# Seven products for eight: the up projection of two token blocks by Strassen's algorithm, and the down projection as a stage of its own

## The chip, the cores and the metric

One NeuronCore of a Trainium2 chip runs the whole program. The metric is the device time of one execution in microseconds (us). The kernel before was run three times: 2574.15, 2579.14 and 2577.27 us, median 2577.27 us.

## What is computed

One inference step of a decoder trunk of two layers. 1088 columns of activations (64 sample tokens of 8 sequences, then 1024 prompt tokens) of 1024 features pass through a mixer (layer 0: mLSTM heads beside a short convolution; layer 1: sliding-window attention) and, in each layer, through a gated ConvFFN. It is the FFN that matters here:

```python
def conv_ffn(h, prev, w_up, conv_w, w_down):
    u = h @ w_up                                  # 1024 -> 2 * 2816
    u, new_prev = causal_conv(u, prev, conv_w)    # depthwise, width 3, along the tokens
    g, a = jnp.split(u, 2, axis=-1)
    return (jax.nn.silu(g) * a) @ w_down, new_prev

x = x + g1 * y                                    # y of the mixer
h = rms_norm(x, norm2[l]) * (1 + sc2) + sh2
y, fp = conv_ffn(h, st_ffn[l], f_w_up[l], f_conv_w[l], f_w_down[l])
x = x + g2 * y
```

## The kernel before

**Number format.** All is float32. An operand of a product is split into a high part (a cast to the type that TensorE, PE, multiplies) and a low part (what the cast left out). A product is three passes: high by high, high by low, low by high (`PASS`). ScalarE (ACT) casts, VectorE (DVE) subtracts: `split` (L81) for activations, `wunit` (L92) for a weight unit of 128 x 1024, which SyncE (SP) has loaded into a staging tile `st` (3 buffers).

**Tiling.** The columns are three blocks, `BLK`: 384, 384 and 320. A feature tile f (0 to 21) has two parts, p = 0 (the gate's input g) and p = 1 (a). `mm_unit` (L148) is one product of a part with a block: 8 k tiles by three passes, 24 matmuls into one PSUM bank.

**The up projection.** `up` (L453) runs one tile and one block. For each part: 24 matmuls, then the halo. The convolution needs the two columns before the block, so the product of block 1 or 2 is written behind two columns that ACT copies from the bank of the block before (L466):

```python
mm_unit(ps[:, h:], c1 - c0, w[p], c0)
if bi < 2:
    halo[p] = bank("up")
    A.copy(out=halo[p][:, 0:2], in_=ps[:, n - 2:n])
```

The bank of the next block can take its product only after this copy. Then ACT scales (L469), DVE adds the two other taps (L485; L475 and L477 for the 64 sample columns of block 0), ACT takes the Silu (L488), DVE multiplies (L489), and `split` makes the operand of the down projection, which stays in SBUF in a tile `g` of all 1088 columns.

**The down projection** comes in between: after each two feature tiles, `down` (L492) adds their part of all eight output tiles m over the three blocks (6 matmuls a group, L501), and `gate_add` (L396, DVE, L403) adds each group times its gate to x, which stays in SBUF. In layer 0 the modulation units of the next layer (`ada`, L198) run between the groups. The last two tiles go block by block, so that the next layer's norm can begin; its blocks 1 and 2 are finished between the products of keys and values (`kv`, L1028).

**Order.** The program lists jobs with the weight units that each takes; units of the coming jobs are loaded and split ahead. A scheduler of the framework then fixes one order of instructions for each engine, which works through it in that order.

Of the kernel before, what the change touches and what calls it, by code (L numbers as in the profile page):

```python
# [17 lines left out]
KT = 8  # L18
# [15 lines left out]
WSLOT = 2048  # L34

# order of the first steps, see trunk()
# [11 lines left out]
def trunk(ctx: ExitStack, tc: tile.TileContext, I, O):  # L48
# [27 lines left out]
    # activations, feature major, as hi and lo parts: the input of each product  # L76
# [3 lines left out]
    # ---------------------------------------------------------------- weights  # L80
# [28 lines left out]
    def fetch(n):  # L109
        """splits units of the coming jobs until n are ready"""  # L110
        while len(ready) < n and fetched[0] < len(jobs):
            srcs = jobs[fetched[0]][0]
            if fetched[1] < len(srcs):
                ready.append(wunit(srcs[fetched[1]]))
                fetched[1] += 1
            else:
                fetched[0] += 1
                fetched[1] = 0
# [29 lines left out]
    def mm_unit(ps, n, w, c0):  # L148
        """ps[:, :n] = sum over the 8 k tiles of w_k^T h_k[:, c0:c0+n]"""
# [6 lines left out]
    def mm_tok(ps, ws, c0, k0=0, k1=KT):  # L156
        """ps = h[:, c0:c0+128]^T times 512 columns of weights"""
# [66 lines left out]
    # modulation units that run between other work, each loaded one turn ahead  # L224
    pend, loaded = [], []

    def later_units(which, tmp):
        for l, cb in which:
            for u, run in enumerate(ada(l, 8 * cb, 16, 8, tmp)):
                pend.append((I["w_ada"][l, cb:cb + 2, u], run))  # L230

    def pump():
# [3 lines left out]
        if pend:  # L236
            src, run = pend.pop(0)
            w = wscratch("wa")
            SY.dma_start(out=w.rearrange("p (u c) -> p u c", u=2), in_=src.rearrange("u p c -> p u c"))
# [7 lines left out]
    def rsqrt_(out, v, tmp):  # L247
        """out = v^-0.5 of v in SBUF (v > 0), refined by one Newton step"""
# [13 lines left out]
    def ring(new, n, uses):  # L262
        """temporaries of 386 columns, n to a tile, a new tile after so many of them"""
# [10 lines left out]
    class Norm:  # L274
        """h = rms(x) * norm * (1 + sc) + sh, block by block"""
# [7 lines left out]
        def square(self, k, bi, eng=None):  # L283
            """adds the squares of x's k tile to the block's sum"""
# [19 lines left out]
        def total(self, bi):  # L304
            """the sums in token major, where the root takes few columns"""
# [20 lines left out]
        def spread(self, bi):  # L326
            """the roots, the same on all partitions"""
# [14 lines left out]
        def sample(self, k, eng):  # L342
            """k tiles k and k + 1 of the sample columns, up to their split"""
# [10 lines left out]
        def apply(self, k, bi):  # L354
            """k tiles k and k + 1 of a block"""
# [1358 lines left out]
```

## Time and profile before

| | us |
|---|---|
| three runs | 2574.15, 2577.27, 2579.14 |
| profiled execution, span | 2578.1 |
| of it TensorE busy | 2516.1 (98%) |
| VectorE / ScalarE / GpSimd busy | 1569.3 / 860.1 / 292.3 |
| moved by DMA | 195.97 MB, 76 GB/s over the span |

The profiled execution is a run of its own; the time that the page gives for it is its span, and it lies between the three measured ones. "Busy" of PE means that a matmul was under way; matmuls are pipelined, so one lasts longer in a row (335 ns) than its distance to the next. A group of instructions has its idle time before it and what released it.

### The profile page before, as it was taken

Reading aid. Unit: us, or ns where it says so; the run is one execution under the profiler, and the core shown is the slowest. Engines: PE = TensorE matmul, PEld = TensorE weight load, DVE = VectorE, ACT = ScalarE, POOL = GpSimd, SP = SyncE. Lnnn points to the kernel's source line nnn. Section 1 sums busy time; section 2 is a strip of 40 time slices with the busy share of each in tenths; the row PEclk is TensorE's granted clock in tenths of the full one; section 3 lists DMA queues with packets and bytes.
Section 4 is the critical chain, followed back from the end, with each engine's and each line's share of the span. In section 5 each row is a group of like instructions: output and inputs, shape, how many; then the busy total and the mean of one; then the engine's idle time right before and its main releaser. Section 6 shows DMA issues by size and latency. Waiting matters only on the chain.

```text
span 2578.1 us, 40693 instructions
## 1 busy us (share of the span) xinstructions
PE 2516.1 (98%) x15899; PEld 2374.7 (92%) x15899; DVE 1569.3 (61%) x3700; ACT 860.1 (33%) x2182; POOL 292.3 (11%) x523
## 2 busy tenths in 40 slices
PE   6999999999999999999998989899999999999999
PEld 5988998999999999999997866699999999999999
DVE  7332326556666656566667788956756666666665
ACT  5102323345222223222225456635422222222231
POOL 2001014121000000000006431203100000000000
PEclk9999999999999999999998999999999999999999
DMA  7455315411322212221110221220111111111112
GB/s 262 164 170 188 116 54 159 144 50 42 99 66 82 82 59 82 74 66 50 41 47 15 85 67 42 70 65 34 50 34 49 50 42 42 50 50 33 50 42 76
DMA packets 78144, 195.97 MB, mean 76 GB/s; under 512 B 9321, under 2 KB 36745, under 8 KB 77409
## 3 DMA queue, kind: packets, MB, share of 16 engines
q1 hardware_dynamic: 72960, 179.65, 21.7%
q0 software_dynamic: 4416, 13.60, 1.4%
q8 instruction: 126, 2.06, 0.3%
q14 instruction: 66, 0.53, 0.1%
q10 hardware_dynamic: 576, 0.13, 0.0%
HBM read 178.55 MB, written 16.76 MB: 76 GB/s over the span
## 4 chain that ended last, share of the span: by engine, by line
PE 86%; DVE 9%; ACT 1%; DMA 1%; issue 1%; POOL 1%; SPq 0%; DVEq 0%; ACTq 0%; POOLq 0%
PE up L152 39%; PE dn L501 20%; PE pj L152 6%; PE op L152 5%; PE cv L152 5%; PE ada L198 2%; PE q L1028 1%; PE kv L1028 1%; PE vp L160 1%; DVE nt L368 1%; DVE p L1207 1%; DVE p L1223 1%; PE op L1134 1%; DVE h L381 1%; DVE n L293 1%
## 5 line engine op out<-in xcount | busy, mean ns | idle before, releaser
L152 PE MATMUL up<-h,w 128*128 128x384 f32 (+1 forms) x6336 | 1052.8, 327 | 0.0
L152 PEld LDWEIGHTS up<-h,w 128*128 128x128 f32 x6336 | 1046.1, 188 | 5.9 <-ACT u L473 5.0
L501 PEld LDWEIGHTS dn<-g,w 128*128 128x128 f32 x3168 | 524.4, 188 | 7.5 <-DVE x L403 4.2
L501 PE MATMUL dn<-g,w 128*128 128x384 f32 (+1 forms) x3168 | 531.0, 327 | 0.0
L485 DVE SCALAR_TENSOR_TENSOR y<-up,fcw,y 128x319 f32<-128x319 f32 (+3 forms) x528 | 300.2, 570 | 228.9 <-ACT y L469 148.4
L403 DVE SCALAR_TENSOR_TENSOR x<-dn,mod,x 128x320 f32<-128x320 f32 (+1 forms) x528 | 300.0, 571 | 123.9 <-PE dn L501 111.0
L95 ACT CAST w<-st 128x1024 fp32r<-128x1024 f32 x179 | 186.5, 1054 | 498.7 <-PE dn L501 373.2
L96 DVE TENSOR_TENSOR w<-st,w 128x1024 fp32r<-128x1024 f32 x179 | 219.2, 1235 | 113.6 <-ACT w L95 111.9
L469 ACT ACTIVATE y<-up,fcw 128x320 f32<-128x320 f32 (+1 forms) x264 | 145.3, 551 | 76.5 <-PE up L152 75.0
L152 PE MATMUL op<-h,w 128*128 128x384 f32 (+1 forms) x960 | 163.4, 331 | 0.0
L152 PEld LDWEIGHTS op<-h,w 128*128 128x128 f32 x960 | 160.3, 193 | 0.0
L82 ACT CAST g<-y 128x384 fp32r<-128x384 f32 x132 | 65.4, 496 | 269.3 <-DVE y L489 269.3
L152 PEld LDWEIGHTS pj<-h,w 128*128 128x128 f32 x864 | 141.9, 188 | 8.4 <-issue 5.0
L152 PE MATMUL pj<-h,w 128*128 128x384 f32 (+1 forms) x864 | 145.1, 327 | 0.0
L152 PEld LDWEIGHTS cv<-h,w 128*128 128x128 f32 x720 | 118.4, 188 | 10.9 <-issue 7.5
L152 PE MATMUL cv<-h,w 128*128 128x384 f32 (+1 forms) x720 | 123.7, 328 | 0.0
L475 DVE TENSOR_SCALAR y<-u,fcw 128x64 f32<-128x64 f32 x88 | 22.5, 256 | 157.5 <-ACT u L473 157.5
L1028 PE MATMUL q<-w,h 128*128 128x512 f32 x432 | 115.4, 408 | 0.6 <-DVE rq L1000 0.6
L479 POOL COPY fst<-u 128x16 f32<-128x16 f32 x88 | 22.8, 259 | 820.3 <-ACT u L473 820.3
L488 ACT ACTIVATE y<-y 128x384 f32<-128x384 f32 x132 | 67.2, 509 | 131.7 <-DVE y L485 68.3
L83 DVE TENSOR_TENSOR g<-y,g 128x384 fp32r<-128x384 f32 x132 | 70.5, 534 | 61.1 <-ACT g L82 61.1
L466 ACT COPY up<-up 128x2 f32<-128x2 f32 x176 | 25.6, 146 | 222.3 <-PE up L152 211.5
(316 smaller groups left out, 2389.3 us busy)
## 6 DMA issues: line engine op xcount, KB each, us to landing
st<-in_f_up SPq DMA_DIRECT2D x88, 512.0 KB, 3.6
wa<-in_w_ada SPq DMA_DIRECT2D x40, 1024.0 KB, 5.6
st<-in_f_down SPq DMA_DIRECT2D x44, 512.0 KB, 3.5
st<-in_w_in SPq DMA_DIRECT2D x22, 512.0 KB, 4.5
st<-in_w_out SPq DMA_DIRECT2D x16, 512.0 KB, 3.7
st<-in_w_qkv SPq DMA_DIRECT2D x12, 512.0 KB, 3.7
wr<-in_w_ada SPq DMA_DIRECT2D x11, 512.0 KB, 8.6
x<-in_xT SPq DMA_DIRECT2D x4, 1088.0 KB, 10.7
```

Source lines behind the costliest of these rows:

```text
L82: A.copy(out=dst_hi, in_=src)
L83: (eng or V).tensor_tensor(out=dst_lo, in0=src, in1=dst_hi.bitcast(F32), op=ALU.subtract)
L95: A.copy(out=w[:, 0, :], in_=s)
L96: V.tensor_tensor(out=w[:, 1, :], in0=s, in1=w[:, 0, :].bitcast(F32), op=ALU.subtract)
L152: PE.matmul(ps[:, :n], w[:, a, 128 * k:128 * k + 128], H[k][:, b, c0:c0 + n], start=(k == 0 and i == 0), stop=(k == KT - 1 and i == 2))
L198: PE.matmul(hold["ps"][32 * c:32 * c + 32, 0:32 * nf], M["c"][:, 9 * kt:9 * kt + 32], wk[:, c], start=(kt == 0), stop=(kt == KT - 1), tile ...
L403: V.scalar_tensor_tensor(out=x[:, o:c1], in0=ps[:, o - c0:n], scalar=gt[:, 0:1], in1=x[:, o:c1], op0=ALU.mult, op1=ALU.add)
L469: A.activation(out=y[:, o:n], in_=ps[:, o:n], func=AF.Copy, scale=cw[:, fi, 2:3])
L485: V.scalar_tensor_tensor(out=y[:, q:n], in0=ps[:, q - d:n - d], scalar=cw[:, fi, j:j + 1], in1=y[:, q:n], op0=ALU.mult, op1=ALU.add)
L488: A.activation(out=a, in_=a, func=AF.Silu)
L501: PE.matmul(ps[:, :c1 - c0], ws[j][:, a, 128 * m:128 * m + 128], gt[f][:, b, c0:c1], start=(j == 0 and i == 0), stop=(j == 1 and i == 2))
L1028: PE.matmul(ps, H[2 * u + k][:, a, c0:c0 + 128], w[:, b, 512 * k:512 * k + 512], start=(u + k + i == 0), stop=(u == 3 and k == 1 and i == 2))
```

## The change

**Strassen.** The input features and the two parts make a 2 x 2 split: even and odd k tiles (two for each of four pairs i), part g and part a; blocks 0 and 1 are the two halves of the columns. For tiles 2 to 21 of each layer, the eight quarter products of that split (12 matmuls each, 96 in all) become seven, 84 matmuls, in the Winograd form. The sums S1 to S4 of the weights are made for every tile, by four GpSimd (POOL) additions of 128 x 512 in place in the staging tile, each with a cast on ACT and a low part on DVE (`sums_a`). The sums T1 to T4 of the activations are made once a layer, while tiles 0 and 1 run plainly (`PLAIN = 2`), and lie in the buffers of x and of the norm's scratch (`sums_b`); x goes to DRAM (`xd`) before and comes back after. The banks X, Y, W and Z collect the seven products: X, W and Z take further products or, through DVE, copies that ACT has kept. Block 2 (320 columns) is computed plainly behind them.

**Down.** The gated products go to DRAM (`gd`, one store a tile and block). When all 22 tiles are done, `ffn_down` runs three blocks by two halves of the output by 11 units: a unit loads 512 KB of weights and two tiles of the block's activations, splits both, and adds 24 matmuls to four banks, which hold the sum over all 22 tiles. So x gets one residual addition for each output tile and block instead of eleven, and the next layer's norm of blocks 0 and 1 runs behind the down products. The modulation units are halved to 512 KB and run every second step.

The core of the diff:

```diff
+        def store(f, bi, yt):
+            a, b = (yt[:, p, h:h + c1 - c0] for p in range(2))
             A.activation(out=a, in_=a, func=AF.Silu)
             V.tensor_tensor(out=a, in0=a, in1=b, op=ALU.mult)
-            split(g[:, 0, c0:c1], g[:, 1, c0:c1], a)
+            SY.dma_start(out=gd[:, f, c0:c1], in_=a)
+
+        def halo(ps, before, bi):
+            n = (2 if bi > 1 else 0) + BLK[bi - 1][1] - BLK[bi - 1][0]
+            A.copy(out=ps[:, 0:2], in_=before[:, n - 2:n])
+
+        def product(out, wt, ht, first=True, last=True):
+            for i in range(4):
+                for k, (a, b) in enumerate(PASS):
+                    PE.matmul(out, wt(i, a), ht(i, b), start=(first and i == 0 and k == 0), stop=(i == 3 and k == 2),
+                              skip_group_check=True)
+            tick()
...
+            y0 = ytile("y")
+            product(x, A11, B11)
+            c1 = kept(x)
+            product(y, A12, B21)
+            add(y, c1)
+            conv(f, 0, 0, Y, y0)
+            product(w, A22, T4)
+            product(x, S[2], T2, first=False)
+            u2 = kept(x)
+            Z = bank("Z")
+            z = Z[:, 2:2 + nb]
+            product(z, S[1], T1)
+            p5 = kept(z)
+            product(x, S[3], T3, first=False)
+            u3 = kept(x)
+            add(w, u3)
+            conv(f, 1, 0, W, y0)
+            store(f, 0, y0)
+            product(z, S[4], B22, first=False)
+            add(x, p5)
+            add(z, u2)
+            after()
+            y1 = ytile("y")
+            for p, (ps, before) in enumerate(((Z, Y), (X, W))):
+                halo(ps, before, 1)
+                conv(f, p, 1, ps, y1)
+            store(f, 1, y1)
+            plain(f, ws, (2,), (Z, X))
...
+    def ffn_down(l, hold, gd, nxt):
...
+                r = dp.tile([128, 2, 384], F32, tag="gr", name=nm("gr"), bufs=2)[:, :, 0:n]
+                SY.dma_start(out=r, in_=gd[:, 2 * u:2 * u + 2, c0:c1])
...
+                for m in range(4):
+                    if u == 0:
+                        acc[m] = bank("dn")
+                    for j in range(2):
+                        for i, (a, b) in enumerate(PASS):
+                            PE.matmul(acc[m][:, :n], w[:, a, 512 * j + 128 * m:512 * j + 128 * m + 128], g[:, b, j, :],
+                                      start=(u == 0 and j == 0 and i == 0), stop=(u == 10 and j == 1 and i == 2))
+                    if u == 10:
+                        gate_add(l, 5, xs, 4 * mh + m, acc[m], bi)
+                        nxt.each(4 * mh + m, bi)
```

`kept` copies a bank to SBUF on ACT, `add` adds such a copy into a bank on DVE; `conv` is the convolution as before (ACT L533, DVE L549, and L539 and L541 for the sample columns of block 0); `after()` makes the weight sums of the next tile. `plain` runs the halo copies (L562), the 24 matmuls (L154) and the convolution for block 2.

How the order of the engines moves, at the place where one tile's block 2 begins. PE before, one feature tile (`up_...` are the banks of the two parts and three blocks, `h` the activations, `w_...` the weights):

```order
L152 MATMUL up_10033<-h,w_9788 128x384 x24
L152 MATMUL up_10070<-h,w_10023 128x384 x24
L152 MATMUL up_10058<-h,w_9788 128x384 x24
L152 MATMUL up_10095<-h,w_10023 128x384 x24
L152 MATMUL up_10136<-h,w_9788 128x320 x24
L152 MATMUL up_10165<-h,w_10023 128x320 x24
```

And PE in the changed kernel, the second half of one Strassen tile (`sw_...` are the sums S, `x_...` and `n_...` the sums T) and its block 2:

```order
L583 MATMUL Z_8203<-n_5345,sw_8039 128x384 x12
L583 MATMUL X_8136<-x_557_5346,sw_8035 128x384 x3
L583 MATMUL X_8136<-x_560_5363,sw_8035 128x384 x3
L583 MATMUL X_8136<-x_578_5590,sw_8035 128x384 x3
L583 MATMUL X_8136<-x_581_5607,sw_8035 128x384 x3
L583 MATMUL Z_8203<-h,sw_8047 128x384 x12
L154 MATMUL up_8289<-h,w_7902 128x320 x24
L154 MATMUL up_8319<-h,w_7907 128x320 x24
```

Before, the two products of block 1 lay one behind the other, so that between a product and the one whose bank takes its halo there was always another; now the last product into Z is followed at once by the one that needs Z's last two columns.

ACT before, from the halo copies of block 0 of part a to the multiplication of block 1:

```order
L466 COPY up_10095<-up_10070 128x2
L469 ACTIVATE y_10032<-up_10070,fcw 128x320
L473 COPY u_10098<-up_10070 128x8x8
L82 CAST g_10031<-y_10032 128x384
L466 COPY up_10136<-up_10058 128x2
L469 ACTIVATE y_10111<-up_10058,fcw 128x384
L488 ACTIVATE y_10111<-y_10111 128x384
L466 COPY up_10165<-up_10095 128x2
L469 ACTIVATE y_10111<-up_10095,fcw 128x384
L82 CAST g_10031<-y_10111 128x384
```

And ACT in the changed kernel from the last cast of the weight sums on (`Z_8203` and `X_8136` are the banks of block 1):

```order
L515 CAST sw_8273<-st_8126 128x512
L562 COPY Z_8203<-Y_8137 128x2
L533 ACTIVATE y_8276<-Z_8203,fcw 128x384
L562 COPY X_8136<-W_8138 128x2
L533 ACTIVATE y_8276<-X_8136,fcw 128x384
L556 ACTIVATE y_8276<-y_8276 128x384
L562 COPY up_8289<-Z_8203 128x2
L562 COPY up_8319<-X_8136 128x2
L533 ACTIVATE y_8288<-up_8289,fcw 128x320
```

The halo copies for block 2 have moved from directly behind the product, ahead of the convolution, to behind the convolution's scaling of both parts and the Silu (L556).

DVE in the changed kernel in the same stretch, from the addition into W (bank of block 0, part a) to the one ahead of that Silu's last input:

```order
L602 TENSOR_TENSOR W_8138<-W_8138,c_8230 128x384
L602 TENSOR_TENSOR X_8136<-X_8136,c_8216 128x384
L516 TENSOR_TENSOR sw_8269<-st_8131,sw_8269 128x512
L539 TENSOR_SCALAR y_8139<-u_8234,fcw 128x64
L549 SCALAR_TENSOR_TENSOR y_8139<-W_8138,fcw,y_8139 128x319
L602 TENSOR_TENSOR Z_8203<-Z_8203,c_8201 128x384
L541 SCALAR_TENSOR_TENSOR y_8139<-u_8234,fcw,y_8139 128x64
L516 TENSOR_TENSOR sw_8273<-st_8126,sw_8273 128x512
L549 SCALAR_TENSOR_TENSOR y_8139<-W_8138,fcw,y_8139 128x318
L541 SCALAR_TENSOR_TENSOR y_8139<-u_8234,fcw,y_8139 128x64
L549 SCALAR_TENSOR_TENSOR y_8276<-Z_8203,fcw,y_8276 128x384
L557 TENSOR_TENSOR y_8139<-y_8139 128x384
```

The next row of DVE is the second L549 on Z; the Silu waits for that. None of the L602 and L516 rows was there before.

## Rows read from the trace of the kernel before

**Rows 1.** The page: the span, TensorE's busy time, the chain that ended last by line.

```profile
span 2578.1 us, 40693 instructions
...
PE 2516.1 (98%) x15899; PEld 2374.7 (92%) x15899; DVE 1569.3 (61%) x3700; ACT 860.1 (33%) x2182; POOL 292.3 (11%) x523
...
PE up L152 39%; PE dn L501 20%; PE pj L152 6%; PE op L152 5%; PE cv L152 5%; PE ada L198 2%; PE q L1028 1%; PE kv L1028 1%; PE vp L160 1%; DVE nt L368 1%; DVE p L1207 1%; DVE p L1223 1%; PE op L1134 1%; DVE h L381 1%; DVE n L293 1%
```

**Rows 2.** Groups by shape: busy us, mean ns of one | idle before, releaser.

```profile
L152 PE MATMUL up<-h,w 128*128 128x384 f32 x4224 | 747.2, 335 | 0.0
...
L466 ACT COPY up<-up 128x2 f32<-128x2 f32 x176 | 25.6, 146 | 222.3 <-PE up L152 211.5 <-issue 10.7
...
L485 DVE SCALAR_TENSOR_TENSOR y<-up,fcw,y 128x384 f32<-128x384 f32 x176 | 108.1, 617 | 151.2 <-ACT y L469 148.4
...
L477 DVE SCALAR_TENSOR_TENSOR y<-u,fcw,y 128x64 f32<-128x64 f32 x176 | 48.6, 276 | 0.0
...
L489 DVE TENSOR_TENSOR y<-y 128x384 f32<-128x384 f32 x88 | 49.2, 559 | 3.6 <-ACT y L488 0.8
...
L575 DVE TENSOR_TENSOR cv<-cv,cv 128x384 f32<-128x384 f32 x6 | 3.3, 558 | 19.3 <-PE cv L152 19.3
...
L83 DVE TENSOR_TENSOR h<-zr,h 128x512 fp32r<-128x512 f32 x8 | 8.9, 1118 | 1.4 <-ACT h L82 1.4
...
L96 DVE TENSOR_TENSOR w<-st,w 128x1024 fp32r<-128x1024 f32 x179 | 219.2, 1235 | 113.6 <-ACT w L95 111.9
...
L488 ACT ACTIVATE y<-y 128x384 f32<-128x384 f32 x88 | 46.3, 526 | 119.9 <-DVE y L477 63.4 <-DVE y L485 56.5
...
L82 ACT CAST g<-y 128x384 fp32r<-128x384 f32 x88 | 45.2, 513 | 174.1 <-DVE y L489 174.1
...
L1002 POOL TENSOR_TENSOR rt<-rt,rq 128x512 f32<-128x512 f32 x18 | 23.9, 1325 | 112.1 <-DVE s L1220 27.5 <-DVE rq L1000 24.8 <-ACT ssq L253 15.6
```

**Rows 3.** PE in order of time, two stretches: start us, us, instructions merged.

```profile
1120.15 47.56 PE L152 MATMUL up<-h,w 128*128 128x384 f32 x288
...
1167.55 23.98 PE L501 MATMUL dn<-g,w 128*128 128x384 f32 x144
...
1376.82 5.53 PE L501 MATMUL dn<-g,w 128*128 128x320 f32 x36
```

**Rows 4.** DVE in order of time in the up stage.

```profile
1196.64 0.54 DVE L485 SCALAR_TENSOR_TENSOR y<-up,fcw,y 128x319 f32<-128x319 f32 x1
...
1197.10 0.28 DVE L477 SCALAR_TENSOR_TENSOR y<-u,fcw,y 128x64 f32<-128x64 f32 x1
```

**Rows 5.** PE in order of time: two gaps, [idle before <- releaser].

```profile
593.47 0.79 PE L335 MATMUL ssq<-ident,r 80*128 80x80 f32 x4 [2.20 <-DVE r L260]
...
1774.42 1.39 PE L316 MATMUL ssq<-ones,n 128*128 128x1 f32 x6 [3.16 <-DVE n L293]
```

**Rows 6.** Windows: length, busy us of PE, PEld, DVE, ACT, POOL, granted clock, DMA, GB/s.

```profile
593.43:596.84 3.41, 3.37 (x13) 3.37 (x14) 2.64 (x6) 2.24 (x7) 0.00 (x0) 0.50 0.00 0
...
1402.39:1416.04 13.65, 9.02 (x27) 6.54 (x28) 12.38 (x38) 7.66 (x24) 10.54 (x17) 0.50 0.04 10
...
1774.45:1781.28 6.83, 6.83 (x27) 6.83 (x28) 3.09 (x8) 0.53 (x3) 1.65 (x4) 0.50 0.46 156
```

**Rows 7.** DMA issues (KB, us to landing), and the window with the most traffic.

```profile
st<-in_f_down SPq DMA_DIRECT2D x44, 512.0 KB, 3.5
...
x<-in_xT SPq DMA_DIRECT2D x4, 1088.0 KB, 10.7
...
od<-ob POOLq DMA_DIRECT2D x8, 256.0 KB, 2.3
...
20.00:40.00 20.00, 14.78 (x304) 11.81 (x305) 18.77 (x51) 13.46 (x33) 2.95 (x3) 1.00 1.04 398
```

**Rows 8.** PE and DVE in order of time at the start of layer 0's FFN.

```profile
573.85 12.47 PE L152 MATMUL up<-h,w 128*128 128x384 f32 x71
...
602.20 2.18 DVE L485 SCALAR_TENSOR_TENSOR y<-up,fcw,y 128x384 f32<-128x384 f32 x4
```

More of the change, by code (lines that the diff above doesn't have):

```diff
@@ L225, in trunk, with later_units @@
     pend, loaded = [], []
[L227 removed]
+    def later_units(which, tmp, nf=16, place=None):
         for l, cb in which:
[L229 to L230 removed]
+            for u, run in enumerate(ada(l, 8 * cb, nf, 8, tmp)):
+                pend.append((I["w_ada"][l, cb:cb + nf // 8, u], run, place or (lambda: wscratch("wa"))))
     def pump():
@@ new lines, in ffn_up, with wq, pair, load @@
+        quarter = lambda e, c0: (lambda i, b: HA[:, 2 * i + e, b, c0:c0 + nb])
+        T1 = lambda i, b: TS[1][:, i, b]
+        T2, T3, T4 = ((lambda i, b, j=j: TS[i, "T"][:, j, b]) for j in range(3))
+        def wq(w, e):
+            return lambda i, a: w[:, a, 128 * (2 * i + e):128 * (2 * i + e) + 128]
+        def pair(f):
+            def load():
+                r = []
+                for p in range(2):
+                    s = stg.tile([128, 1032], F32, tag="st", name=nm("st"))[:, 0:1024]
+                    SY.dma_start(out=s, in_=I["f_up"][l, f + NF * p])
+                    w = wtile()
+                    A.copy(out=w[:, 0, :], in_=s)
+                    V.tensor_tensor(out=w[:, 1, :], in0=s, in1=w[:, 0, :].bitcast(F32), op=ALU.subtract)
+                    r.append((w, s.rearrange("p (i e c) -> p e i c", e=2, c=128)))
+                return r
+            return load
@@ new lines, in sums_a, with put @@
+        def sums_a(ws):
+            (_, g), (_, a) = ws
+            a11, a12, a21, a22 = g[:, 0], g[:, 1], a[:, 0], a[:, 1]
+            out = {}
+            def put(j, dst, x, y, op):
+                G.tensor_tensor(out=dst, in0=x, in1=y, op=op)
+                t = hold["pool"].tile([128, 2, 4, 128], F32R, tag="sw", name=nm("sw"), bufs=4)
+                A.copy(out=t[:, 0], in_=dst)
+                V.tensor_tensor(out=t[:, 1], in0=dst, in1=t[:, 0].bitcast(F32), op=ALU.subtract)
+                out[j] = lambda i, b: t[:, b, i, :]
+            put(3, a11, a11, a21, ALU.subtract)
+            put(1, a21, a21, a22, ALU.add)
+            put(2, a22, a22, a11, ALU.subtract)
+            put(4, a12, a12, a22, ALU.subtract)
+            return out
@@ new lines, in conv @@
+            if bi == 2:
+                A.copy(out=pst[:, fi, :], in_=ps[:, n - 2:n])
+            for j in (1, 0):
+                d = 2 - j
+                q = o if bi else P0 + d
+                V.scalar_tensor_tensor(out=y[:, q:n], in0=ps[:, q - d:n - d], scalar=cw[:, fi, j:j + 1],
+                                       in1=y[:, q:n], op0=ALU.mult, op1=ALU.add)
+        def store(f, bi, yt):
+            c0, c1 = BLK[bi]
+            h = 2 if bi else 0
+            a, b = (yt[:, p, h:h + c1 - c0] for p in range(2))
@@ L553, in ffn, with plain @@
-        down(NF - 2)
+            SY.dma_start(out=gd[:, f, c0:c1], in_=a)
+        def halo(ps, before, bi):
+            n = (2 if bi > 1 else 0) + BLK[bi - 1][1] - BLK[bi - 1][0]
+            A.copy(out=ps[:, 0:2], in_=before[:, n - 2:n])
+        def plain(f, ws, blocks, before=None):
+            for bi in blocks:
+                c0, c1 = BLK[bi]
+                h = 2 if bi else 0
+                yt = ytile("y")
+                now = []
+                for p in range(2):
+                    ps = bank("up")
+                    if bi:
+                        halo(ps, before[p], bi)
+                    mm_unit(ps[:, h:], c1 - c0, ws[p][0], c0)
+                    conv(f, p, bi, ps, yt)
+                    now.append(ps)
+                before = now
+                store(f, bi, yt)
@@ new lines, in product, with strassen, kept, add @@
+        def product(out, wt, ht, first=True, last=True):
[4 more added lines that the diff above has]
+            tick()
+        nextS = {}
+        def strassen(f, ws, after):
+            A11, A12, A22 = wq(ws[0][0], 0), wq(ws[0][0], 1), wq(ws[1][0], 1)
+            S = nextS.pop(f)
+            B11, B21, B22 = quarter(0, b0), quarter(1, b0), quarter(1, d0)
+            X, Y, W = bank("X"), bank("Y"), bank("W")
+            x, y, w = X[:, 2:2 + nb], Y[:, 0:nb], W[:, 0:nb]
+            def kept(ps):
+                c = ctile("c")
+                A.copy(out=c, in_=ps)
+                return c
+            def add(ps, c):
+                V.tensor_tensor(out=ps, in0=ps, in1=c, op=ALU.add)
+            y0 = ytile("y")
[26 more added lines that the diff above has]
+            plain(f, ws, (2,), (Z, X))
@@ new lines, in job_of, with go, after @@
+        def job_of(f):
+            def go(ws):
+                hold["next"] = None
+                if f < PLAIN:
+                    plain(f, ws, range(3))
+                    assert not later
+                    for i in range(4 * f // PLAIN, 4 * (f + 1) // PLAIN):
+                        sums_b(i)
+                    after()
+                else:
+                    strassen(f, ws, after)
+            def after():
+                if PLAIN <= f + 1 < NF:
+                    fetch(1)
+                    nextS[f + 1] = sums_a(ready[0])
+            job([pair(f)], go, 2)
```

217 lines of the change are left out of this document (115 added, 102 removed).

## The prediction, made before the changed kernel was run

> **What bounds the kernel now.** I read the page first: TensorE (PE) is busy for 2516.1 of 2578.1 us, and the chain that ended last lies on it for most of the span, 39% in the up products and 20% in the down products [rows 1]. Then the groups by shape: the up matmuls of 384 columns show no idle time ahead of them, and the little copy of two halo columns (L466) waits for PE, not PE for it [rows 2]. So the FFN is a stream of matmuls with nothing between, and a matmul taken out is worth its slot. The slot comes from the order of PE in time: two feature tiles with both parts, 288 matmuls, start at 1120.15 and the next piece at 1167.55, so 23.7 us a tile; 36 matmuls of 320 columns in 5.53 us are about 0.150 us each; what is left of the 23.7 is (23.7 - 48 x 0.150) / 96 = 0.172 us for one of 384 [rows 3]. The third thing to see is what an idle PE costs besides the idle time: after gaps of 2.20 and 3.16 us [rows 5] the granted clock shows 0.50, the lower of the two levels, for 3.41 and 6.83 us [rows 6]; while it does, PE does half its work.
>
> **The sum** is made against the span of 2578.1 us; the median of the three runs is 2577.27 us, so both stand for the same time.
>
> *Products, removed.* In 40 of 44 feature tiles (20 a layer) blocks 0 and 1 take 7 products of 12 matmuls for 96 matmuls: 40 x 12 x 0.172 = **-83 us**. The Trainium skill, "TensorE: Matmul & The Clock Gate", section "Back-to-back issue gap", gives N/2.4 + 2.5 ns, 162.5 ns for 384 columns, and says itself that this is for a single gap and counts too much at large N; here the row is larger, not smaller, and by the page's figure this term would be -78 us. The row is used.
>
> *The halo of block 2, a new wait.* Before, the copy of the two columns stood on ScalarE (ACT) right behind the product it reads, and one whole product of 24 matmuls (4.1 us) lay on PE between the two. Now PE has the last product (Z += S4 B22) and then at once block 2, whose first matmul waits for the copy into its bank. On ACT that copy stands behind the Silu of block 1 (L556), and the Silu behind the second convolution step on Z, which VectorE (DVE) reaches at the end of a queue of 13 operations that starts with the add into W (L602, the first row of DVE's piece of the order). PE works in order, so nothing of it can run in that time. From the end of the last product (0): the product before it ended 12 x 0.172 = 2.06 us earlier, its copy takes 0.51 (as L82), so DVE starts at -1.55. One DVE operation follows another 0.08 us sooner than its length says (0.54 long, 0.46 to the next, [rows 4]). With that: two adds of 384 at 0.48 each (0.558, L575), a weight part of 512 at 0.61 (0.69, between 0.559 of 384 and 1.235 of 1024), 0.20 and 0.46, at 0.68; the add into Z to 1.16; then 0.20, 0.61, 0.46, 0.20, 0.54, 0.48 to 3.65; the last step 0.62 to 4.27; the Silu 0.53 and the copy 0.15 [rows 2]: 4.95 us. Three hand-overs between engines and the adds into PSUM, which no row shows, put it a little higher: I take 5.2. Lower bound 4.2 (all hand-overs free, adds in PSUM as short as those of SBUF less the overlap); upper 6.5 (the two weight parts at 1.118, the slow row of that size [rows 2]). 40 x 5.2 = **+208 us** (168 to 260).
>
> *The clock after it.* The gap is longer than those of [rows 5], and PE did up to 21.6 us of unbroken work before each. I take 3.41 us at 0.50 each time, the shorter of the stretches seen, so 1.7 us lost: 40 x 1.7 = **+68 us**. Ends: 0 (the clock stays) and 136 (6.83 us each time).
>
> *The sums of the activations.* They are made while tiles 0 and 1 run plainly, and DVE is the long one: eight adds of 768 columns (7.2), 32 operations of 384 (15.4), four weight splits of 1024 (4.6) and six of 512 (3.6), and the convolutions of the same time (15.4) are 46 us. DVE is free of the norm at 602.20, so the last sum is there at about 648. PE starts tile 0 at 573.85 [rows 8], needs 47.4 us for two tiles and some 5 for the norm's gap and slow clock that are there today, and comes to the part of the third product that reads the last sum at about 632. So 16 us of waiting; some of it runs in the shadow of work I have put in twice, and I take 15 for each layer: **+30 us** (10 to 44).
>
> *From up to down.* Down reads the gated products from DRAM, and its first load waits for the last store. After the last up matmul: ACT's scaling 0.5, two convolution steps and the product about 1.6, with a weight split of 1.1 on DVE between them, in all about 3.6; the store 2.3 and the load 3.5 (nearest rows: 256 KB from SBUF to DRAM, 512 KB to SBUF [rows 7]); cast and split of 768 columns 0.8 + 0.95. That is 11 us, and 1.7 for the clock: 2 x 12.7 = **+25 us** (16 to 40).
>
> *Down itself.* The same 3168 matmuls, 24 a step. A step of 4.1 us loads 512 KB of weights and 384 KB of activations, 220 GB/s, and in layer 0 with the modulation units about 285; 398 were moved in the first slices of the program [rows 7]. DVE has 2.2 us of splits in a step, ACT 1.9. Hidden: **0** (up to +56, below). 240 of 264 residual adds a layer fall away from DVE, which costs and brings nothing, as PE never waited for them.
>
> *Start of the attention.* Today block 1's and 2's norm is finished between the products for keys and values: 13.65 us at clock 0.50 with 9.02 us of PE work [rows 6], so 4.6 us idle and 4.5 lost. Now blocks 0 and 1 are normed behind down, and only block 2 is left: **-9 us** (0 to -9).
>
> Sum: -83 + 208 + 68 + 30 + 25 - 9 = **+239 us**, 2578 + 239 = **2817 us**, 9% slower. ScalarE, GpSimd and the weight loads have room in a tile of 28 us and are put at nothing. SyncE's rows rise from 370 to 754, above all by the 132 stores and 132 loads of the products and x to DRAM and back in 16 parts of 1.1 MB; a store waits for its product and holds up the weight loads queued behind it, which have a whole tile of time. x is needed again at the first residual add, 45 us into down, and lands in about 10.7 us [rows 7]. The four GpSimd adds of a tile's weights wait for the second weight split, which is done before the first product, and take 4 x 1.33 us (L1002, [rows 2]) of the 12 us that lie ahead of the products that read them.
>
> **Rivals.**
> 1. *Faster.* The wait is short because the copy follows the add into Z at once: 0.5 for the add and 0.15 for the copy, 0.7 us, and no lower clock after so short a gap. Then -83 + 28 + 30 + 25 - 9 = -9 us, **2569 us**. It decides below 0.9 us a tile. For it: the copy needs only the add. Against it: the order of each engine is fixed in the program, and there the Silu stands in front. 4 in 100.
> 2. *The wait without the clock.* 2817 - 68 = **2749 us**. For it: gaps of 0.6 to 1.9 us today are often followed by full clock. Against: none of 2.2 us or more is. 12 in 100.
> 3. *The clock stays low twice as long* (6.83 us as after 1774.42, [rows 5, 6]): 2817 + 68 = **2885 us**. 14 in 100.
> 4. *DVE and GpSimd slow each other.* A DVE operation of 512 columns took 1.118 us in one place, where 0.69 lie on the line of the others [rows 2]. If two operations of the chain each wait out a GpSimd add, 2 x 1.33 us a tile: +106, **2923 us**; against it, the adds are over by then. The Trainium skill, "SBUF — State Buffer", section "Who interferes with whom", says that a DVE operation with two inputs in SBUF and a GpSimd one that reads SBUF exclude each other for a whole instruction; by that rule the weight parts in the chain would be those hit. 7 in 100.
> 5. *Down is bound by its loads in layer 0*, where the modulation units come on top: 0.85 us more in each of 66 steps, +56, **2873 us**. 7 in 100.
> 6. *The change doesn't do what it says.* The matmuls are counted in the order, 480 fewer; only a stall of PE elsewhere that vanishes with them could give no change. 1 in 100.
>
> **How the numbers follow.** The forecast has 55 in 100, from 2760 to 2880 by the ends of its wait. All but rivals 1 and 6 end slower. The range that leaves out rivals 1, 6 and the ends of 3, 4 and 5 is 2690 to 2920 us. About 0.2% (5 us) is what a measurement of this kernel can tell from no change: faster by more than that 0.05, within it 0.01, slower 0.94.
>
> **What would show it.** Right: in the order of PE in time, every Strassen tile has one gap of about 5 us ahead of the first block 2 matmul, put down to ACT's halo copy, and the clock row of the up stages falls to 0.9 or so; the group of the block 2 matmuls carries some 200 us of idle time; the page shows one gap of 10 us or more at each start of down. The 384-column matmuls of the up stage fall by 480. Wrong: if these gaps are under 1 us, or if the up stage shows no gap and the down stage does.

## The result, and the profile after

The changed kernel takes 2869.31 us (median of 4 runs, 2864.25 to 2873.19), the kernel before in the same comparison 2578.2 us. The ratio is **1.1128, 95% interval 1.1111 to 1.1146**: 11% slower. The prediction was 2817 us with a range of 2690 to 2920.

The page of the changed kernel, to be read beside [rows 1]: the span, the engines' busy time, the granted clock in 40 slices, the chain by line.

```profile
span 2871.4 us, 41313 instructions
...
PE 2555.4 (89%) x15547; PEld 2391.5 (83%) x15547; DVE 1674.8 (58%) x3392; ACT 1162.4 (40%) x2620; POOL 523.9 (18%) x683
...
PEclk9999999988999998989999999998899989989999
...
PE dn L698 19%; PE up L154 15%; PE X L583 9%; PE pj L154 5%; PE cv L154 4%; DVE y L549 3%; PE W L583 3%; PE Z L583 3%; PE Y L583 3%; PE op L154 2%; PE q L1190 2%; PE kv L1190 2%; PE ada L200 2%; PE vp L162 1%; DVE sw L516 1%
```

PE is busy for 89% of the span where it was for 98%. It has 39 us more of busy time beside 352 matmuls fewer (480 fewer in the up stages, 128 more because the halved modulation units take twice as many); some of them must have run slowly. The clock row has eight 8s, all in the two up stages and where down begins; that of the kernel before has one. The groups by shape (busy us, mean ns of one | idle before, releaser) show where the idle time is:

```profile
L154 PE MATMUL up<-h,w 128*128 128x320 f32 x2112 | 407.6, 364 | 200.9 <-ACT up L562 200.9
...
L154 PE MATMUL up<-h,w 128*128 128x384 f32 x384 | 75.4, 357 | 22.4 <-ACT up L562 22.4
...
L698 PE MATMUL dn<-gh,w 128*128 128x384 f32 x2112 | 378.1, 339 | 24.4 <-ACT gh L83 24.4
...
L516 DVE TENSOR_TENSOR sw<-st,sw 128x512 fp32r<-128x512 f32 x160 | 111.0, 694 | 103.5 <-ACT sw L515 103.5
```

The matmuls of block 2 (320 columns) had no idle time ahead of them before; now they have 200.9 us, all put down to ACT's halo copy (L562), 192 of them in the Strassen tiles. The 384-column ones of tiles 0 and 1 have 22.4, the down products 24.4.

By stage, from the start of each in PE's order of time, in us (before, then after):

| | before | after | difference |
|---|---|---|---|
| 40 Strassen tiles | 23.70 each | 28.82 each | +204.8 |
| the rest of the up stages (start of both layers) | 4.9 lost each | 34.3 and 35.3 lost | +59.8 |
| PE idle ahead of down's first matmul | none | 12.46 and 12.3 | +24.8 |
| down with the modulation units, to the end | 283.0 and 266.2 | 289.75 and 267.7 | +8.2 |
| attention and output projection | 402.5 | 398.1 | -4.4 |
| sum | | | +293.2 |

The spans differ by 2871.4 - 2578.1 = 293.3 us. The 28.82 are the mean of 19 tiles of layer 1, from one first block 2 matmul (2034.85) to the last (2582.37); layer 0 has 28.75. In the kernel before, up and down lie between each other: its down is what is left of an FFN's time without 22 x 23.70 and the 4.9. The idle time ahead of down counts from the end of the last up matmul's own slot, 0.16 us before its recorded end.

One Strassen tile in PE's order of time (start us, us, merged matmuls, [idle before <- releaser]): the first of the seven products, the last, block 2, the next tile.

```profile
714.19 2.27 PE L583 MATMUL X<-h,w 128*128 128x384 f32 x12
...
726.77 2.25 PE L583 MATMUL Z<-h,sw 128*128 128x384 f32 x12
...
733.83 10.05 PE L154 MATMUL up<-h,w 128*128 128x320 f32 x48 [4.81 <-ACT up L562]
...
743.72 2.25 PE L583 MATMUL X<-h,w 128*128 128x384 f32 x12
```

The same gap stands in 38 of the 40 tiles, at 4.81 or 4.82 us (4.57 in the last tile of each layer); counted from the last product's nominal end it is 4.97 (733.83 - 728.86). On ACT in that stretch: the copy of the sixth product, the halo of block 1, the Silu, and the halo copy that block 2 waits for.

```profile
726.97 0.48 ACT L598 COPY c<-X 128x384 f32<-128x384 f32 x1 [1.12 <-PE X L583]
...
730.23 0.14 ACT L562 COPY Z<-Y 128x2 f32<-128x2 f32 x1 [0.51 <-DVE Z L602]
...
733.20 0.52 ACT L556 ACTIVATE y<-y 128x384 f32<-128x384 f32 x1 [0.96 <-DVE y L549]
...
733.63 0.16 ACT L562 COPY up<-Z 128x2 f32<-128x2 f32 x1
```

And on DVE the first operation of its queue, the addition into Z, and the last step that the Silu waits for:

```profile
727.49 0.57 DVE L602 TENSOR_TENSOR W<-W,c 128x384 f32<-128x384 f32 x1 [0.91 <-ACT c L598]
...
729.65 0.55 DVE L602 TENSOR_TENSOR Z<-Z,c 128x384 f32<-128x384 f32 x1
...
732.55 0.61 DVE L549 SCALAR_TENSOR_TENSOR y<-Z,fcw,y 128x384 f32<-128x384 f32 x1
```

That is the chain of the forecast, step by step: DVE starts 1.4 us before the last product ends (forecast 1.55), Z is complete at 730.2, and then 3.4 us pass in which the copy's data lie ready and the copy stands behind the Silu. The clock, in windows of the seven products, of block 2 in this tile and of block 2 in the next (length, busy us of PE, PEld, DVE, ACT, POOL, granted clock, DMA, GB/s):

```profile
714.19:728.86 14.67, 14.67 (x86) 14.51 (x84) 8.43 (x15) 6.68 (x15) 5.35 (x7) 1.00 0.03 11
...
733.83:743.72 9.89, 9.89 (x49) 9.89 (x49) 3.30 (x5) 2.15 (x5) 0.02 (x1) 0.69 0.20 75
...
763.34:772.02 8.68, 8.68 (x48) 8.68 (x49) 3.30 (x5) 2.15 (x5) 0.30 (x1) 0.80 0.19 74
```

The products run at 1.00, block 2 behind the gap at 0.69 and 0.80, that is, worked out from the mean, at the lower level, 0.50, for 6.1 and 3.5 us of it; its 48 matmuls take 9.89 and 8.68 us instead of 7.1.

### The profile page after: what moved, and what is told of

Its sections match the earlier page's. It is cut to its first block, busy times and chain, and to the rows that moved or that the text cites. A ratio compares the mean times of both kernels' runs of the same rounds, so it can differ in the third digit from the quotient of the medians.

```text
span 2871.4 us, 41313 instructions
## 1 busy us (share of the span) xinstructions
PE 2555.4 (89%) x15547; PEld 2391.5 (83%) x15547; DVE 1674.8 (58%) x3392; ACT 1162.4 (40%) x2620; POOL 523.9 (18%) x683
## 4 chain that ended last, share of the span: by engine, by line
PE 74%; DVE 16%; issue 5%; ACT 3%; DMA 2%; POOL 1%; SPq 0%; ACTq 0%; DVEq 0%; POOLq 0%
PE dn L698 19%; PE up L154 15%; PE X L583 9%; PE pj L154 5%; PE cv L154 4%; DVE y L549 3%; PE W L583 3%; PE Z L583 3%; PE Y L583 3%; PE op L154 2%; PE q L1190 2%; PE kv L1190 2%; PE ada L200 2%; PE vp L162 1%; DVE sw L516 1%
## 5 line engine op out<-in xcount | busy, mean ns | idle before, releaser
L154 PE MATMUL up<-h,w 128*128 128x320 f32 (+1 forms) x2496 | 482.3, 363 | 223.2 <-ACT up L562 223.2
L154 PEld LDWEIGHTS up<-h,w 128*128 128x128 f32 x2496 | 468.9, 232 | 237.4 <-ACT up L562 237.4
L698 PE MATMUL dn<-gh,w 128*128 128x384 f32 (+1 forms) x3168 | 536.4, 329 | 24.4 <-ACT gh L83 24.4
L698 PEld LDWEIGHTS dn<-gh,w 128*128 128x128 f32 x3168 | 525.5, 189 | 37.7 <-ACT gh L83 25.0
L549 DVE SCALAR_TENSOR_TENSOR y<-up,fcw,y 128x320 f32<-128x320 f32 (+2 forms) x208 | 114.9, 554 | 286.7 <-ACT fpst L545 267.5
L84 DVE TENSOR_TENSOR gh<-gr,gh 128x768 fp32r<-128x768 f32 (+1 forms) x132 | 122.8, 932 | 220.6 <-ACT gh L83 220.1
L513 POOL TENSOR_TENSOR st<-st,st 128x512 f32<-128x512 f32 x120 | 157.9, 1316 | 441.8 <-DVE w L501 438.3
L583 PE MATMUL X<-x,sw 128*128 128x384 f32 x960 | 186.2, 343 | 1.7 <-DVE x L84 1.7
L583 PEld LDWEIGHTS X<-x,sw 128*128 128x128 f32 x960 | 171.7, 191 | 4.1 <-DVE x L84 3.1
L533 ACT ACTIVATE y<-up,fcw 128x320 f32<-128x320 f32 (+1 forms) x104 | 55.2, 533 | 294.5 <-PE up L154 284.9
L516 DVE TENSOR_TENSOR sw<-st,sw 128x512 fp32r<-128x512 f32 x160 | 111.0, 694 | 103.5 <-ACT sw L515 103.5
L154 PE MATMUL op<-h,w 128*128 128x384 f32 (+1 forms) x960 | 163.3, 331 | 0.0
L154 PEld LDWEIGHTS op<-h,w 128*128 128x128 f32 x960 | 160.2, 193 | 0.0
L154 PEld LDWEIGHTS pj<-h,w 128*128 128x128 f32 x864 | 141.9, 188 | 8.4 <-issue 5.0
L154 PE MATMUL pj<-h,w 128*128 128x384 f32 (+1 forms) x864 | 145.1, 327 | 0.0
L556 ACT ACTIVATE y<-y 128x384 f32<-128x384 f32 x132 | 67.0, 507 | 149.7 <-DVE y L541 97.4
L154 PEld LDWEIGHTS cv<-h,w 128*128 128x128 f32 x720 | 118.4, 188 | 10.9 <-issue 7.5
L154 PE MATMUL cv<-h,w 128*128 128x384 f32 (+1 forms) x720 | 123.7, 328 | 0.0
```

Source lines behind the costliest of these rows:

```text
L84: (eng or V).tensor_tensor(out=dst_lo, in0=src, in1=dst_hi.bitcast(F32), op=ALU.subtract)
L154: PE.matmul(ps[:, :n], w[:, a, 128 * k:128 * k + 128], H[k][:, b, c0:c0 + n], start=(k == 0 and i == 0), stop=(k == KT - 1 and i == 2))
L513: G.tensor_tensor(out=dst, in0=x, in1=y, op=op)
L516: V.tensor_tensor(out=t[:, 1], in0=dst, in1=t[:, 0].bitcast(F32), op=ALU.subtract)
L549: V.scalar_tensor_tensor(out=y[:, q:n], in0=ps[:, q - d:n - d], scalar=cw[:, fi, j:j + 1], in1=y[:, q:n], op0=ALU.mult, op1=ALU.add)
L556: A.activation(out=a, in_=a, func=AF.Silu)
```

## The experiments

Theory A is that of the prediction: PE waits for a copy that comes too late in ACT's order, and pays a second time in clock. All kernels are edits of the changed kernel. fill_gap, halo_early_pin and halo_plain ran twice, the others four or five times.

**The copy behind the product.** The halo columns are not read by the matmuls; only their place in the bank made block 2 wait.

```diff
                     ps = bank("up")
-                    if bi:
-                        halo(ps, before[p], bi)
                     mm_unit(ps[:, h:], c1 - c0, ws[p][0], c0)
+                    if bi:
+                        halo(ps, before[p], bi)
```

> Edit: the changed kernel, but the two halo columns are copied into the bank of the next block behind its product instead of ahead of it, so no matmul waits for the copy. Theory A (the time was lost because block 2's first matmul waited for a copy that stands behind the Silu on ACT, 4.97 us a tile, and about 2.0 us of slow clock after it): a Strassen tile takes 14.7 + 7.2 = 21.9 us instead of 28.8, 40 x 6.9 = 278 us come back, and up to 36 more from the same waits in tiles 0 and 1: 2869 - 278 - (0 to 36), so 2555 to 2591 us. Rival B (the wait only hid that DVE is the bound: some 18 us of work a tile and the GpSimd adds beside it): tiles of about 23.5 us with new gaps of PE put down to DVE, 2869 - 213 = 2655 us.

Measured: 2556.31 us, 0.9904 of before (0.9883 to 0.9925). All of the loss in the Strassen tiles is gone; the kernel is now 1% faster than before. A tile in PE's order of time, its start, the first matmuls of block 2 and the start of the next:

```profile
703.80 2.27 PE L583 MATMUL X<-h,w 128*128 128x384 f32 x12
...
714.27 1.92 PE L154 MATMUL up<-h,w 128*128 128x320 f32 x12
...
725.47 2.27 PE L583 MATMUL X<-h,w 128*128 128x384 f32 x12
```

21.67 us a tile (725.47 - 703.80), 2.03 below the 23.70 of before: 40 x 2.03 = 81 us, the seven products' worth. (Most of the later tiles take 21.72, by which it is 79 us.) Of the 313 us that came back the Strassen tiles give some 284; the rest comes from the start of the layers, since this edit moves the copies of tiles 0 and 1 as well. The scheduler now puts a part of block 2 between two products, which it may, since nothing holds it. DVE is not the bound, as rival B had it: in 100 us of the up stage it works for 76.78 and PE does not stop once:

```profile
700.00:800.00 100.00, 100.00 (x610) 100.00 (x609) 76.78 (x146) 51.90 (x126) 35.96 (x39) 1.00 0.24 81
```

**Matmuls in the gap.** This holds the wait and takes away the idle PE.

```diff
             product(z, S[4], B22, first=False)
+            fill = bank("fill")
+            for i in range(28):
+                tc.keep_in_program_order(PE.matmul(fill[:, 0:nb], ws[0][0][:, 0, 0:128], HA[:, i % 8, 0, b0:b1], ...))
             add(x, p5)
```

> Edit: the changed kernel, with 28 matmuls of 384 columns into a spare bank between the last product of a Strassen tile and block 2; nothing reads them. They take 28 x 0.172 = 4.8 us, so PE works through the 4.97 us of the wait. Theory A says that the wait costs twice, idle time and a slower clock after it: the idle time is still lost, but block 2 runs at full clock, 9.2 -> 7.2 us, 40 x 2.0 = 80 us less: 2789 us, granted clock 1.00 through the up stage. Rival C (the lower clock in block 2 is not caused by the idle PE, or costs nothing): within 10 us of 2869 us, clock as before.

Measured: 2792.92 us, 1.0831 of before (1.0808 to 1.0854), 76 us less than the changed kernel though PE does 1120 matmuls more. In PE's order of time, and the window of block 2:

```profile
726.35 5.04 PE L625 MATMUL fill<-h,w 128*128 128x384 f32 x28
...
731.32 7.30 PE L154 MATMUL up<-h,w 128*128 128x320 f32 x48
```

```profile
731.32:738.46 7.14, 7.14 (x49) 7.14 (x49) 3.30 (x5) 2.14 (x5) 0.03 (x1) 1.00 0.24 86
```

Block 2 runs at 1.00 in 7.14 us. So of the 7.1 us that a Strassen tile loses against 21.7, 2.0 are the clock (28.82 less 26.78 from one block 2 to the next here) and 5.1 the wait: shown, not argued.

**The copy early, PE's order held.**

```diff
             add(z, u2)
+            ahead2 = [bank("up"), bank("up")]
+            halo(ahead2[0], Z, 2)
+            halo(ahead2[1], X, 2)
...
-            plain(f, ws, (2,), (Z, X))
+            plain(f, ws, (2,), None, ahead2)
```

The first matmul of block 2 and of the next tile are held behind the one before them in the program, so that the scheduler doesn't move other products into the gap.

> Edit: the changed kernel, but the halo copies for block 2 stand on ACT directly behind the additions into Z and X, ahead of block 1's convolution; PE's order is held as it was (last product, block 2, next tile). Theory A: the gap falls from 4.97 to the addition into Z and the copy, which DVE reaches in the midst of its queue: about 1.6 us, 40 x 3.4 = 135 us less. After so short a gap the clock may or may not fall: 2735 us if it falls as now, 2655 us if it stays. Rival B (what PE waits for is DVE's queue as a whole, not the copy's place): a gap of over 4 us stays, over 2820 us.

Measured: 2658.32 us, 1.0309 of before (1.0286 to 1.0332). Two tiles and 100 us of the up stage:

```profile
722.16 7.30 PE L154 MATMUL up<-h,w 128*128 128x320 f32 x48 [1.41 <-ACT up L564]
...
745.52 7.31 PE L154 MATMUL up<-h,w 128*128 128x320 f32 x48 [1.41 <-ACT up L564]
```

```profile
700.00:800.00 100.00, 94.35 (x574) 93.07 (x573) 71.53 (x134) 49.36 (x115) 25.73 (x34) 1.00 0.23 77
```

The gap is 1.41 us, and the clock stays at 1.00: of the two cases the second. A wait of this length still costs 40 x 1.7 us (a tile is 745.52 - 722.16 = 23.36 us) of what the products save. The tile is 0.33 us shorter than before even so; what keeps this kernel slower is what the change adds elsewhere, at the start of each layer and of down. Over all Strassen tiles but the first of each layer (675 to 1119 us and 1925 to 2368) the granted clock is 1.00 too.

**No Strassen.** The down stage by itself: all tiles plain, without the sums of the activations, the halo behind the product as above. x still goes to DRAM and back.

```diff
-PLAIN = 2
+PLAIN = 22
...
-                    for i in range(4 * f // PLAIN, 4 * (f + 1) // PLAIN):
-                        sums_b(i)
```

> Edit: all 22 tiles of a layer run plainly (24 matmuls for each part and block, no sums), the halo copied behind the product; the rest as changed: products to DRAM, down as its own stage. It shows the price of the down stage alone. Theory A (down is not bound by its loads; only the start of down, 12.3 us of gap and 2 us of slow clock, is added, and the start of the attention gives 4 us back): 2578 + 2 x 14.5 - 4 = 2603 us. Rival D (the stage costs more than its start, by loads or by DVE): over 2630 us.

Measured: 2609.55 us, 1.0119 of before (1.0099 to 1.0138). PE's waits in this run (in total, times, longest) have one row for down:

```profile
PE dn L699 <- ACT gh L83: 23.5, 2, 12.4
```

The stage costs some 31 us over before, where 25 were expected. Its loads don't bind it: apart from the start, PE does not wait there. By itself the stage gains nothing; whether Strassen's products could do without it was not tried. Against halo_behind it says what Strassen's products are worth net: 2609.55 - 2556.31 = 53 us, of the 81 that the tiles give; the rest goes into the sums at the start of each layer and a longer wait at the start of down (14.4 and 15.1 us there).

**The halo behind the product in tiles 0 and 1 only.** The up stage loses more at its start than the prediction had. In the changed kernel, PE there:

```profile
604.30 15.18 PE L154 MATMUL up<-h,w 128*128 128x320 f32 x78 [4.09 <-ACT up L562]
...
629.95 14.02 PE L154 MATMUL up<-h,w 128*128 128x384 f32 x72 [10.47 <-ACT up L562]
...
658.33 1.01 PE L583 MATMUL W<-x,w 128*128 128x384 f32 x2 [1.33 <-DVE x L84]
```

Two of these gaps, 4.09 and 10.47 us, are halo copies of the plain tiles, and only the small ones, like the third, wait for the sums (L84, `x_...`).

```diff
-                    if bi:
+                    if bi and f >= PLAIN:
                         halo(ps, before[p], bi)
                     mm_unit(ps[:, h:], c1 - c0, ws[p][0], c0)
+                    if bi and f < PLAIN:
+                        halo(ps, before[p], bi)
```

> Edit: the changed kernel, with the halo copied behind the product in the plain tiles 0 and 1 of each layer only; in the Strassen tiles it stays ahead of block 2. It takes apart the 30 us that the first four tiles of each layer lose. Theory A (some 19 of them are halo waits of the plain tiles, gaps of 0.7, 4.1 and 10.5 us and slow clock after, and some 11 the sums of the activations): 2869 - 2 x 19 = 2831 us. Rival E (all of it is DVE's work on the sums, and the wait only moves to the first Strassen tile): above 2855 us.

Measured: 2847.14 us, 1.104 of before (1.1018 to 1.1063), 22 us less where 38 were expected and under 14 by rival E. PE at the start of layer 0:

```profile
598.77 32.90 PE L154 MATMUL up<-h,w 128*128 128x384 f32 x201
...
648.33 1.80 PE L585 MATMUL Z<-n,sw 128*128 128x384 f32 x3 [6.06 <-ACT n L83]
...
669.47 10.04 PE L154 MATMUL up<-h,w 128*128 128x320 f32 x48 [4.82 <-ACT up L562]
```

The plain tiles are clean (201 matmuls in one piece), but the first Strassen tile now waits for the sums, 6.06 us in one place. So the two overlap: behind some 16 of the 38 us of the plain tiles' halo waits lay DVE's work on the sums, which would have been waited for in any case. In halo_behind the same sums cost less, since the 48 matmuls of block 2 run in that place (from 638.82 to 646.20 us there).

**The start of down.** In the changed kernel:

```profile
1244.48 19.05 PE L698 MATMUL dn<-gh,w 128*128 128x384 f32 x96 [12.30 <-ACT gh L83]
```

PE is idle for 12.30 us, and the 96 matmuls behind it take 19.05 us instead of 16.5, at the lower clock at first. Two edits on top of halo_behind: eleven tensors in DRAM instead of one, and the first units in buffers that outlive the up stage. They were made together, so that the runs do not say what each gives.

```diff
-        gd = drm.tile([128, NF, T], F32, tag=f"gd{l}", name=f"gd{l}")
+        gd = [drm.tile([128, 2, T], F32, tag=f"gd{l}_{u}", name=f"gd{l}_{u}") for u in range(NF // 2)]
...
+                first = bi == 0 and mh == 0 and u < 2
+                if first:
+                    r = stg.tile([128, 1032], F32, tag="st", name=nm("st"))[:, 0:768].rearrange("p (j c) -> p j c", j=2)
...
+                    g = wpl.tile([128, WSLOT], F32R, tag="w", name=nm("w"))[:, 0:1536].rearrange("p (a j c) -> p a j c", a=2, j=2)
```

> Edit: halo behind the product everywhere, and the start of down taken apart: the products in DRAM are 11 tensors of two feature tiles each, so that a load waits only for its own stores, and the activations of the first two units of down go into the staging and weight buffers, which are free before the up stage ends. Theory A (PE is idle for 14.4 and 15.1 us at the start of down because the first load waits for the last store): two units, 8.3 us of matmuls, run in that gap, 2 x 8.3 us less and up to 5 us of slow clock: 2556 - 17 to - 22, so 2534 to 2540 us, the gap at the third unit 4 to 7 us. Rival F (the weights of down or the DMA queue are late as well): a gap ahead of the first unit stays, 2550 to 2560 us.

Measured: 2542.07 us, 0.9859 of before (0.9844 to 0.9874), 14 us less than halo_behind and a little above the 2534 to 2540 expected. The first two units run at once behind the up products, and the gap has moved to the third:

```profile
1072.45 8.51 PE L705 MATMUL dn<-w,w 128*128 128x384 f32 x48
...
1090.33 4.88 PE L705 MATMUL dn<-gh,w 128*128 128x384 f32 x15 [9.36 <-DMA gr<-gd]
```

It is 9.36 us, not 4 to 7: the third unit's load still waits, now by name for the DMA (`gr<-gd`). Its buffer lies where the buffers of the up stage were, which is the likely reason; that was not tried by itself. With `u < 3`:

> Edit: as early_units2, with the third unit's activations in those buffers too; they come free while the first two units run. Theory A: the gap at the third unit of 4 to 7 us closes for the most part: 4 to 8 us less than early_units2, 2528 to 2534 us. Rival F: the third unit waits for a buffer that the first one holds, no change against early_units2.

Measured: 2537.87 us, 0.9847 (0.983 to 0.9863). The median is 4 us below that of early_units2, but the intervals overlap, so this step alone is not settled by the runs; 2528 to 2534 were expected. The idle time is shown to be shorter:

```profile
1080.58 4.76 PE L705 MATMUL dn<-w,w 128*128 128x384 f32 x24 [0.48 <-ACT w L83]
...
1088.24 1.65 PE L705 MATMUL dn<-gh,w 128*128 128x384 f32 x4 [2.91 <-ACT gh L83]
```

**Three plain tiles**, on top of early_units2:

```diff
-PLAIN = 2
+PLAIN = 3
```

> Edit: as early_units2, with three plain tiles in each layer instead of two, so that the sums of the activations are spread over three. Two tiles more run plainly, 2 x 2.1 = 4 us. Theory A (what is left at the start of a layer, about 11 us, is DVE's work on the sums): most of it is hidden behind the third tile, 2 x 8 us less, so 12 us below early_units2. Rival G (the start is lost to the norm that goes before, which both kernels have): 4 us above early_units2.

Measured: 2528.87 us, 0.9805 (0.979 to 0.9819), 13 us below early_units2 where 12 were expected, though two tiles more do without Strassen. The plain tiles run through, and block 2 of the first Strassen tile covers what is left of the sums:

```profile
596.69 56.61 PE L154 MATMUL up<-h,w 128*128 128x384 f32 x345
...
661.90 1.62 PE L154 MATMUL up<-h,w 128*128 128x320 f32 x10
...
666.27 0.51 PE L583 MATMUL W<-x,w 128*128 128x384 f32 x2
```

**Together:** halo behind the product, three early units, three plain tiles.

> Edit: halo behind the product everywhere, three plain tiles a layer for the sums, and the first three units of down in the staging and weight buffers: plain3 and early_units3 together. Theory A (the terms are independent): plain3's 2529 less the 4 us that early_units3 had on early_units2: 2525 us, 2% below the kernel before. Rival: the third early unit and the third plain tile save the same wait, no change against plain3, 2529 us.

Measured: **2522.76 us, 0.9778 of before (0.9763 to 0.9792)**, from 5 runs. Its interval touches that of plain3, so what the third early unit adds there is not settled. With the three repairs the change is worth 2.2%, and something is left: PE still waits 3.4 and 3.5 us in one place at the two starts of down. The page of this run:

```profile
span 2519.2 us, 41299 instructions
...
PE 2448.9 (97%) x15571; PEld 2304.1 (91%) x15571; DVE 1644.2 (65%) x3376; ACT 1141.1 (45%) x2604; POOL 560.9 (22%) x675
```

## Why the prediction was right

The direction, the cause and the place were right, and the time was low by 52 us. Point by point, by the terms of the sum:

- *Products, -83.* Measured -79 to -81 (halo_behind's tiles), so 0.165 to 0.169 us for one matmul, near the row's 0.172.
- *The wait for the halo, +208.* Measured 40 x 5.1 = 204. The queue of 13 DVE operations, the Silu and the copy follow each other in the trace as in the working; the order of the instructions and durations from before were enough. The weight parts took 0.694 us each, as taken from between two rows (0.69), not the 1.118 of the upper end.
- *The clock, +68.* Measured 40 x 2.04 = 82 (fill_gap). The stretch at 0.50 was the shorter or the longer one of [rows 6] by turns, less what of it fell into the gap itself. Rivals 2 (0) and 3 (3.4 a tile) fall; 2.04 lies between the forecast's 1.7 and rival 3. What the prediction says against rival 2, that no gap of 2.2 us or more is followed by full clock today, is a misreading: one of 4.29 us is, shown in the last section, and one of 2.33 us at 471.27. That the clock would fall was less sure than it was made out to be.
- *The sums of the activations, +30.* This is **the term that failed**: the start of the layers cost +59.8. The prediction had it as DVE's sums alone, 15 a layer, met at the third product. What it left out is that the plain tiles run through the same reordered code, with the halo copy ahead of the product and behind the convolution, the very wait that it had priced for the Strassen tiles: 4.09 and 10.47 us there. halo_plain shows that the copies cost 11 us a layer over what the sums would have cost anyway; without them some 38 us of the 60 are left for both layers, not far from the 30.
- *From up to down, +25.* Measured 24.8 idle and, with the clock at 0.50 for 4.1 and 3.4 us of the first down matmuls, 3.7 of slow clock, so 28.5.
- *Down, 0.* About 4.5 us beyond that slow clock, nearly all in layer 0 (289.75 for 283.0), where the modulation units now run in 32 steps instead of 16; not traced further. Rival 5 falls: PE's order shows no wait for loads within it.
- *Start of the attention, -9.* Measured -4.4. The norm's stretch is gone, but a new wait stands behind it: 5.01 us for DVE ahead of the transposes of the keys, which had no idle time ahead of them before, and a granted clock of 0.50 for 6.83 us after it. The prediction has no term for it.

The wait and the clock of that last term, in the changed kernel:

```profile
1573.85 0.69 PE L1200 MATMUL kTp<-ident,rt 128*128 128x128 f32 x2 [5.01 <-DVE rt L1175]
```

```profile
1572.80:1579.63 6.83, 5.78 (x15) 4.62 (x16) 4.83 (x24) 1.09 (x5) 2.68 (x5) 0.50 0.64 222
```

Together -81 + 204 + 82 + 60 + 28.5 + 4.5 - 4.4 = 293.6, the spans' 293.3.

Rival 1 said that the change pays if the wait is below 0.9 us a tile. halo_early_pin has 1.41 and is slower than before, halo_behind has none and is faster: both on the side that the rival gave, but that is partly luck. By the measured terms the other four come to 60 + 28.5 + 4.5 - 4.4 = 89 us, more than the products' 81, so that without any wait in the Strassen tiles the change would still be some 8 us slower (an estimate). halo_behind is faster because its edit also removed the waits of tiles 0 and 1. Rival 4 (DVE and GpSimd) did not occur in the chain, where no GpSimd addition ran; it occurs elsewhere, below.

## What to carry to other kernels

Where an algorithm saves matmuls, look first at what stands between the last product and the next one: here one small copy behind a Silu took back three and a half times what the seven products save (7.1 us a tile against 2.0). In such a case write what a matmul does not read (here two neighbouring columns of its bank) after it, not before it. And when a wait has been found in new code, look for every other place that runs the same code.

## What was not expected of the hardware

**In these traces a DVE step that takes its inputs from SBUF alone waits out a GpSimd addition that began before it; one with an input in PSUM does not.** In the changed kernel the 64-column step L541 (`u` and `y`, both in SBUF) has a mean of 430 ns, for 276 of the same step before [rows 2]. It is two kinds: 36 of the 176 overlap a GpSimd addition of the weights (L513) and take 1.03 to 1.05 us, the others 0.27. DVE in order of time, and GpSimd in the same microseconds:

```profile
720.23 0.54 DVE L549 SCALAR_TENSOR_TENSOR y<-Y,fcw,y 128x319 f32<-128x319 f32 x1
...
720.68 1.04 DVE L541 SCALAR_TENSOR_TENSOR y<-u,fcw,y 128x64 f32<-128x64 f32 x1
...
722.11 0.27 DVE L541 SCALAR_TENSOR_TENSOR y<-u,fcw,y 128x64 f32<-128x64 f32 x1
```

```profile
720.35 1.30 POOL L513 TENSOR_TENSOR st<-st,st 128x512 f32<-128x512 f32 x1
```

The first L549, which reads PSUM and SBUF, takes its 0.54 us in the midst of that addition; the L541 behind it ends within 0.1 us of the addition's end (720.35 + 1.30). All 36 of these L549 that overlap an addition take 0.54 us, as the 4 that don't. In halo_behind, where the order has moved the additions, 2 overlaps of L541 are left and its mean is 286. But there the step ahead of it, L539, meets them: it multiplies `u` by a column of factors, so it has one tensor as its input, and 31 of its 88 take 0.45 to 1.29 us, most of them 1.28, for 0.25 without an overlap:

```profile
709.72 1.28 DVE L539 TENSOR_SCALAR y<-u,fcw 128x64 f32<-128x64 f32 x1
```

```profile
708.01 2.94 POOL L513 TENSOR_TENSOR st<-st,st 128x512 f32<-128x512 f32 x2
```

It ends 0.05 us after the second addition. The Trainium skill, "SBUF — State Buffer", section "Who interferes with whom", states that a DVE instruction with two SBUF inputs contends with a GpSimd one that reads SBUF, and that one with at most one does not as long as it is outside the 2-port modes, which `tensor_scalar`, the operation of L539, can enter. The trace agrees for L541 and L549; whether L539 ran in such a mode no row shows. No run here separates the cases by an edit made for it. It costs this kernel nothing on the path: PE runs on through the window above without a stop (14.67 of 14.67 us).

**A gap of 1.41 us in every tile left the clock at 1.00, one of 4.97 us brought it to 0.50 in every tile.** What lies between was not tried in this form. Single gaps do not sort by their length alone: in the kernel before, those of 2.20 and 3.16 us are followed by 0.50 [rows 5, 6], and this one of 4.29 us by 1.00 (the window from 20 to 40 us of [rows 7]):

```profile
23.26 1.08 PE L198 MATMUL ada<-raw,cs 128*32 128x64 f32 x32 [4.29 <-DMA raw<-in_w_ada]
```
